# Two-layer streaming encoder on one core: how the relative-bias rows reach HBM, how they are read back, and when the constants are loaded

## The chip, the core and the metric

The kernel runs on one core of a Trainium2 chip. The core has five engines that run side by side: TensorE (PE in the profile, with its weight loads as PEld), VectorE (DVE), ScalarE (ACT), GpSimd (POOL) and SyncE (SP). Sixteen DMA engines move data between HBM and the on-chip memory; the kernel hands them transfers from SP, ACT and POOL, and the profile counts each issuer as a queue (q1 for SP, q0 for POOL, q10 for ACT). The metric is the device time of one execution in microseconds (us).

## What is computed

Two layers work on 256 tokens of width 2048. Each makes one wide input projection, three groups of attention heads, and an output projection that is added to `x`. Group C, the differential attention, has the relative-position bias that this change is about: four heads, one 32-entry table per head, the same table in both layers.

```python
for l in range(DEPTH):                                   # 2 layers
    h = _rms_norm(x, norm_g[l])
    proj = jnp.einsum('bsd,dn->bsn', h, w_in[l])         # 2048 -> 7238 columns
    ...                                                  # groups A (6 heads), B (6 heads)
    # group C, 4 heads, per block of 128 queries q0..q1_
    rel = jnp.arange(q1_)[None, :] - jnp.arange(q0, q1_)[:, None]
    bias = jnp.transpose(rel_bias[_t5_bucket(rel)], (2, 0, 1))
    mask = _chunk_mask(q0, q1_)                          # chunks of 64 tokens
    s1 = einsum(q1, k1) * scale + bias
    s2 = einsum(q2, k2) * scale + bias
    w = softmax(where(mask, s1, -inf)) - lam * softmax(where(mask, s2, -inf))
    ...
    x = x + jnp.einsum('bsm,md->bsd', mixed, w_out[l])
return _rms_norm(x, final_norm_g)
```

The bias depends only on key minus query, so one row of 511 values per head holds all of it. A tile of 128 queries needs that row shifted by one element from partition to partition.

## The kernel before

**Weights.** The weights (about 154 MB over both layers) stream once through the core. They are packed in HBM in the order of use, cut into parts of 512 KB (some of 384 or 454 KB). `load_to` issues each part's transfer from SP into a ring of four `raw` buffers; `split_to` turns a part into a high half `whi` (ACT, L146) and a low half `wlo` (DVE, L147), in rings of five buffers. `take()` hands the next part to the matmuls, and `after()` splits ahead and calls `tick()`, which runs the small steps that `later(n, ...)` has put off by n parts. So the order of all work is fixed by the order of the parts, `layer_slots()`: `n0` (8 parts), `cq0`..`cq3`, `ckv0`, `ckv1`, then head after head of group A as `aq`, `ak`, `ag`, then `n1`, group C as `dq`, `dk`, group B, and `wo0`..`wo15`. SP's transfer of part i waits until part i-4 has been split, since they share a buffer.

**Start.** `x` (2 MB) is loaded in pieces between the first eight parts (`load_start`, L160), and becomes `h` by `chunk_hi` (ACT, L293) and `chunk_lo` (DVE, L296). The first product is `pjL0n` (L392 to L394). Nine dummy matmuls, `ps_idle` (L232), run before it. In `split_start` POOL issues four transfers of constants: `cst` (512 KB: masks, identity, triangle, rotary tables), `rowt` (12 numbers copied to 128 partitions), `relt` (the bias table) and `onet` (which table entry each distance has, 64 KB). They stand under the fourth and eighth part in program order, but nothing precedes them on POOL. First users: `ps_st` (L304) reads a column of `cst`, `post_n0` (L472) reads `rowt`, and `rel_task` (L318) reads `relt` and `onet`.

**Bias rows.** `rel_task`, put off by 21 parts, multiplies `relt` by `onet` into a 4x512 tile, negates it (`relrow`, L320) and has POOL write it to the HBM tensor `reld` 128 times for each head. The source of that transfer lies in four partitions, one for each head. `relative(h)`, called from `post_dq`, later reads `reld` into a 128x384 tile in two transfers (columns 0 to 128 for the first block of queries, 128 to 384 for the second) with a row step of 511, so that each partition is one element further left. Two memsets on POOL then write the masked corners. `scores` adds the two column ranges (`BLK`) to the products on DVE (L748). `decay` is the same for group A and builds its tile on DVE.

Of the kernel before, what the change touches and what calls it, by code (L numbers as in the profile page):

```python
# [10 lines left out]
F32 = mybir.dt.float32  # L11
# [5 lines left out]
P = 128  # L17
D = 2048
S = 256
# [3 lines left out]
NA, NB, NC = 6, 6, 4  # L23
# [4 lines left out]
BIG = 1.0e30  # L28
# [59 lines left out]
BLK = ((0, slice(0, 128)), (1, slice(128, 384)))  # L88
# [7 lines left out]
def trunk(ctx: ExitStack, tc: tile.TileContext, xT, ws, cols, rows, relw, csts, oneh, out):  # L96
    nc = tc.nc
# [4 lines left out]
    tp = ctx.enter_context(tc.tile_pool(name="tmp", bufs=2))  # L102
    dr = ctx.enter_context(tc.tile_pool(name="dr", bufs=1, space=bass.MemoryType.DRAM))
# [7 lines left out]
    V, A, G, T = nc.vector, nc.scalar, nc.gpsimd, nc.tensor  # L111
# [6 lines left out]
    def load_to(r):  # L118
        while st["load"] <= min(r, len(PARTS) - 1):
            i = st["load"]  # L120
            off, w = PARTS[i]
            t = wp.tile([P, MAXW], F32, tag="raw", name=f"raw{i}", bufs=RB)
            src = ws[off:off + P * w].rearrange("(p f) -> p f", p=P)
            n = 2 if i == 0 else 1
            for j in range(n):
                if i < 8:
                    load_start(i, j, n)
                c = slice(j * w // n, (j + 1) * w // n)
                nc.sync.dma_start(out=t[:, c], in_=src[:, c])
            raw_t[i] = t  # L130
            st["load"] += 1

    def split_to(j):
        while st["split"] <= min(j, len(PARTS) - 1):
            i = st["split"]
            w = PARTS[i][1]
            load_to(i)
            hi = wp.tile([P, MAXW], F32R, tag="whi", name=f"whi{i}", bufs=HB)
            lo = wp.tile([P, MAXW], F32R, tag="wlo", name=f"wlo{i}", bufs=HB)
            src = raw_t.pop(i)[:, :w]  # L140
            n = 2 if i == 0 else 1
            for j in range(n):
                if i < 8:
                    split_start(i, j, n)
                c = slice(j * w // n, (j + 1) * w // n)
                A.activation(hi[:, c], src[:, c], AF.Copy)  # L146
                V.tensor_tensor(out=lo[:, c], in0=src[:, c], in1=hi[:, c].bitcast(F32), op=ALU.subtract)  # L147
            if 5 <= i < 10:
                square_start(i - 5)
            half_t[i] = (hi, lo)  # L150
            load_to(i + RB)
            st["split"] += 1
# [11 lines left out]
    def square_start(i):  # L164
        q = [x0[:, 4 * j:4 * j + 4, :] for j in range(4)]
        if i < 4:
            A.activation(q[i], q[i], AF.Square)
            if i % 2:
                V.tensor_tensor(out=q[i - 1], in0=q[i - 1], in1=q[i], op=ALU.add)
        else:  # L170
            V.tensor_tensor(out=q[0], in0=q[0], in1=q[2], op=ALU.add)
            V.tensor_tensor(out=x0[:, 0:2, :], in0=x0[:, 0:2, :], in1=x0[:, 2:4, :], op=ALU.add)
            V.tensor_tensor(out=x0[:, 0, :], in0=x0[:, 0, :], in1=x0[:, 1, :], op=ALU.add)
            X_now.sq = x0[:, 0, :]

    def split_start(i, j, n):
        for c in range(2 * i + j, 2 * i + j + 2 // n):
            xc = x0[:, c, :]
            X_now.chunk_hi(c, xc)
            X_now.chunk_lo(c, xc)  # L180
        if i == 3:
            G.dma_start(out=cst, in_=csts)
            G.dma_start(out=rowt, in_=rows[:, :2 * NA].to_broadcast([P, 2 * NA]))
        elif i == 7:
            G.dma_start(out=relt, in_=relw)
            G.dma_start(out=onet, in_=oneh)


    clock = [0]
# [2 lines left out]
    def later(dt, fn):  # L192
        tasks.append((clock[0] + dt, fn))
# [15 lines left out]
    def take():  # L209
        j = nexth[0]  # L210
        nexth[0] += 1
        split_to(j)
        return half_t.pop(j)

    def after():
        split_to(nexth[0] - 1 + HB - 1)
        tick()
# [3 lines left out]
    cst = const.tile([P, NCST], F32, name="cst")  # L221
    rowt = const.tile([P, 2 * NA], F32, name="rowt")
    relt = const.tile([32, NC], F32, name="relt")
    onet = ap_.tile([32, 512], F32, tag="rb", name="onet")
# [19 lines left out]

    x1d = dr.tile([KC // 4, P, 1024], F32, name="x1d")
    cumd = dr.tile([NA, S], F32, name="cumd")
    reld = dr.tile([NC, P, 512], F32, name="reld")

    def load_x(l, g, eng):
        t = ap_.tile([P, 4, S], F32, tag="v", name=f"xg{l}_{g}", bufs=3)  # L250
# [65 lines left out]
    def rel_task():  # L316
        p = psm.tile([P, 512], F32, tag="psm", name="ps_rel")
        T.matmul(p[:NC, :], lhsT=relt, rhs=onet, start=True, stop=True)  # L318
        t = ap_.tile([NC, 512], F32, tag="v", name="relrow", bufs=3)
        A.activation(t, p[:NC, :], AF.Copy, scale=-1.0)  # L320
        G.dma_start(out=reld, in_=t.unsqueeze(1).to_broadcast([NC, P, 512]))

    def lam_task():
        lamt = ap_.tile([P, 2 * 4 * 64], F32, tag="v", name="lamt", bufs=3)
# [16 lines left out]
    class Layer:  # L341
# [224 lines left out]
            self.post_k("a", h, ps)  # L566

        def relative(self, h):
            self.bias["d", h] = b = tp.tile([P, 384], F32, tag="dec", name=f"rel{self.n}{h}")
            base = reld[:]  # L570
            for c0, n, first in ((0, 128, 255), (128, 256, 127)):
                G.dma_start(out=b[:, c0:c0 + n],
                            in_=bass.AP(base.tensor, base.offset + h * P * 512 + first, [[511, P], [1, n]]))
            G.memset(b[0:64, 64:128], BIG)
            G.memset(b[0:64, 320:384], BIG)

        def post_dq(self, h, ps):
            self.relative(h)
# [131 lines left out]


        def decay(self, h):
            self.bias["a", h] = b = tp.tile([P, 384], F32, tag="dec", name=f"dec{self.n}{h}")
            cq = [self.cumq[:, t, h:h + 1] for t in range(2)]
            rows = self.cumb[:, h % 3, :]
            for o, t, k in ((0, 0, 0), (256, 1, 128)):
                V.scalar_tensor_tensor(out=b[:, o:o + P], in0=rows[:, k:k + P], scalar=cq[t], in1=maskA,
                                       op0=ALU.subtract, op1=ALU.add)
            V.tensor_scalar(out=b[:, P:2 * P], in0=rows[:, 0:P], scalar1=cq[1], scalar2=None, op0=ALU.subtract)
            if h == 2:  # L720
                self.cum_rows(3)

        def scores(self, grp, h, qk, hi, lo):

            n = f"{self.n}{grp}{h}"
            rows = [slice(0, 64), slice(64, 128)] if grp == "d" else [slice(0, P)]
            if grp == "b":
                bias = (maskB[:, P:], maskB)
            else:
                b = self.bias.pop((grp, h))  # L730
                bias = [b[:, c] for _, c in BLK]
            ss, ms = [], []
            for i, r in enumerate(rows):
                ps = pss.tile([P, 512], F32, tag="pss", name=f"pss{n}_{i}")
                prods = [(0, qk[r, 0:P], qk[r, S:S + P])]
                for a, b in ((hi, hi), (hi, lo), (lo, hi)):
                    prods.append((1, a[r, 0:P], b[r, P:384]))
                if grp == "b":
                    prods.insert(1, (0, self.qrT[:, h // 2, :], self.krT[:, h % 2, :]))
                    for a, b in ((self.qrh, self.krh), (self.qrh, self.krl), (self.qrl, self.krh)):  # L740
                        prods.append((1, a[:, h // 2, :], b[:, h % 2, :]))
                for j, (t, a, b) in enumerate(prods):
                    T.matmul(ps[:, BLK[t][1]], lhsT=a, rhs=b, start=(j == 0 or prods[j - 1][0] != t),
                             stop=(j + 1 == len(prods) or prods[j + 1][0] != t))
                s = tp.tile([P, 384], F32, tag=f"s{i}", name=f"s{n}_{i}")
                m = tp.tile([P, 2], F32, tag=f"nm{i}", name=f"nm{n}_{i}")
                for t, c in BLK:
                    V.tensor_tensor_reduce(out=s[:, c], in0=ps[:, c], in1=bias[t], scale=1.0, scalar=FLT_BIG,  # L748
                                           op0=ALU.add, op1=ALU.min, accum_out=m[:, t:t + 1])
                ss.append(s)  # L750
                ms.append(m)
            later(1, lambda: self.exps(grp, h, ss, ms))
# [151 lines left out]
    for l in range(L):  # L904
        lay = Layer(l, X_now)
        go = []
        later(9, lambda: go.append(lay.stat()))
        later(10, lambda: go.pop()())
        if l == 0:
            later(15, lam_task)  # L910
            later(21, rel_task)
        for name in layer_slots():
            if name == "wo0":
                lay.begin_out()
            lay.run(name)
        X_now = lay.xn
# [101 lines left out]
```

## Time and profile before

| | us |
|---|---|
| median of 3 runs | 933.56 |
| range of the runs | 931.06 to 933.9 |
| the profiled execution, its own time | 934.17 |
| span of its trace, first to last instruction | 932.4 |

| engine | busy us | share of the span |
|---|---|---|
| PE | 903.6 | 97% |
| PEld | 797.2 | 86% |
| DVE | 617.3 | 66% |
| ACT | 482.5 | 52% |
| POOL | 206.3 | 22% |

Times in the trace count from the span's first instruction. 1.8 us of the execution lie outside the span. A matmul's busy time is modelled and overlaps the next one's, so a stretch is better judged by where PE's instructions start and by the idle time in front of them than by its busy share. [...]

### The profile page before, as it was taken

What the parts mean: (1) busy time and instruction counts of PE and PEld (TensorE: products, weight loads), DVE (VectorE), ACT (ScalarE), POOL (GpSimd) and SP (SyncE); (2) the same over time, 40 slices, a digit from 0 to 9 for tenths busy, and PEclk for the clock granted to TensorE, in tenths of its full rate; (3) what the DMA queues carried; (4) which work ended last, traced back from release to release, by engine and by line L of the source; (5) the groups of instructions that cost most, each with busy time, mean ns of one, the idle gap of its engine ahead of it and who ended that gap; (6) DMA issues with size and microseconds to landing.
All of it is one profiled execution on the core that took longest, in us unless ns stands there. A gap on an engine that the chain in (4) does not pass through costs nothing.

```text
span 932.4 us, 14297 instructions
## 1 busy us (share of the span) xinstructions
PE 903.6 (97%) x5267; PEld 797.2 (86%) x5267; DVE 617.3 (66%) x1137; ACT 482.5 (52%) x877; POOL 206.3 (22%) x294
## 2 busy tenths in 40 slices
PE   8999589999999999999999999999999999999994
PEld 6888479888888999888888888988888899988884
DVE  5877266675676776777766676667567677676554
ACT  6554244444555665644555554445445566565441
POOL 1151000000412320346542400000041232032220
PEclk8999889999999999999999999999999999999997
DMA  9556455555664445677664555665456545565542
GB/s 312 189 188 145 92 166 196 190 177 159 195 197 152 136 152 177 214 217 232 209 223 163 195 168 163 194 194 175 157 195 195 162 136 141 180 218 209 191 170 90
DMA packets 51429, 168.13 MB, mean 180 GB/s; under 512 B 6724, under 2 KB 9296, under 8 KB 51360
## 3 DMA queue, kind: packets, MB, share of 16 engines
q1 hardware_dynamic: 45888, 154.65, 52.0%
q0 software_dynamic: 4112, 11.37, 4.3%
q10 hardware_dynamic: 1360, 1.21, 0.4%
q8 instruction: 41, 0.67, 0.3%
q14 instruction: 28, 0.23, 0.1%
HBM read 161.95 MB, written 5.26 MB: 179 GB/s over the span
## 4 chain that ended last, share of the span: by engine, by line
PE 93%; DMA 4%; DVE 1%; POOL 0%; ACT 0%; SPq 0%; issue 0%; DVEq 0%; ACTq 0%
PE pjL0wo L376 6%; PE pjL1wo L376 6%; DMA raw<-in_ws 4%; PE pjL0wo L378 3%; PE pjL1wo L378 3%; PE pjL1bg L376 2%; PE pjL0bg L376 2%; PE pjL1ag L376 2%; PE pjL1ak L376 2%; PE pjL1aq L376 2%; PE pjL0ag L376 2%; PE pjL1n L394 2%; PE pjL0n L393 2%; PE pjL1n L392 2%; PE pjL1n L393 2%; PE pjL0n L394 2%
## 5 line engine op out<-in xcount | busy, mean ns | idle before, releaser
L147 DVE TENSOR_TENSOR wlo<-raw,whi 128x1024 fp32r<-128x1024 f32 (+4 forms) x303 | 362.5, 1206 | 129.0 <-ACT whi L146 125.5
L146 ACT ACTIVATE whi<-raw 128x1024 fp32r<-128x1024 f32 (+4 forms) x303 | 301.2, 1012 | 38.9 <-DMA raw<-in_ws 36.6
L624 POOL TENSOR_TENSOR m<-mL,m 128x256 fp32r<-128x256 f32 x32 | 29.1, 913 | 326.6 <-ACT m L623 326.6
L376 PE MATMUL pjL0wo<-m,whi 128*128 128x512 f32 x256 | 91.0, 400 | 0.1
L376 PE MATMUL pjL1wo<-m,whi 128*128 128x512 f32 x240 | 83.8, 393 | 0.1
L378 PE MATMUL pjL0wo<-m,wlo 128*128 128x256 f32 x256 | 71.9, 281 | 0.0
L378 PE MATMUL pjL1wo<-m,wlo 128*128 128x256 f32 x240 | 67.2, 280 | 0.0
L376 PEld LDWEIGHTS pjL0wo<-m,whi 128*128 128x128 f32 x256 | 48.1, 188 | 12.5 <-POOL m L624 0.7
L376 PEld LDWEIGHTS pjL1wo<-m,whi 128*128 128x128 f32 x240 | 44.9, 187 | 10.4 <-POOL m L624 0.7
L378 PEld LDWEIGHTS pjL0wo<-m,wlo 128*128 128x128 f32 x256 | 48.4, 189 | 0.0
L378 PEld LDWEIGHTS pjL1wo<-m,wlo 128*128 128x128 f32 x240 | 45.4, 189 | 0.0
L376 PE MATMUL pjL0ak<-h,whi 128*128 128x512 f32 x96 | 35.8, 411 | 6.1 <-ACT whi L146 6.1
L376 PE MATMUL pjL0ag<-h,whi 128*128 128x512 f32 x96 | 36.7, 420 | 3.7 <-ACT whi L146 3.7
L392 PE MATMUL pjL0n<-whi,h 128*128 128x454 f32 (+2 forms) x96 | 37.1, 386 | 2.7 <-ACT whi L146 2.7
L393 PE MATMUL pjL0n<-wlo,h 128*128 128x454 f32 (+2 forms) x96 | 37.0, 385 | 0.4 <-DVE wlo L147 0.4
L394 PE MATMUL pjL0n<-whi,h 128*128 128x454 f32 (+2 forms) x96 | 36.3, 379 | 0.0
L392 PE MATMUL pjL1n<-whi,h 128*128 128x454 f32 (+2 forms) x96 | 35.3, 368 | 0.0
L394 PE MATMUL pjL1n<-whi,h 128*128 128x454 f32 (+2 forms) x96 | 35.0, 365 | 0.0
L393 PE MATMUL pjL1n<-wlo,h 128*128 128x454 f32 (+2 forms) x96 | 34.9, 364 | 0.0
L376 PE MATMUL pjL1bg<-h,whi 128*128 128x512 f32 x96 | 34.6, 401 | 0.0
L376 PE MATMUL pjL0bg<-h,whi 128*128 128x512 f32 x96 | 34.5, 400 | 0.0
L376 PE MATMUL pjL1ag<-h,whi 128*128 128x512 f32 x96 | 34.3, 400 | 0.0
(563 smaller groups left out, 2433.9 us busy)
## 6 DMA issues: line engine op xcount, KB each, us to landing
raw<-in_ws SPq DMA_DIRECT2D x248, 512.0 KB, 4.1
raw<-in_ws SPq DMA_DIRECT2D x32, 384.0 KB, 3.4
raw<-in_ws SPq DMA_DIRECT2D x15, 454.0 KB, 5.0
xg<-in_xT POOLq DMA_DIRECT2D x4, 512.0 KB, 4.3
x1d<-xg POOLq DMA_DIRECT2D x4, 512.0 KB, 6.2
xg<-x1d POOLq DMA_DIRECT2D x4, 512.0 KB, 3.9
x<-in_xT SPq DMA_DIRECT2D x7, 256.0 KB, 7.2
cumbL<-cumd POOLq DMA_DIRECT2D x4, 384.0 KB, 4.9
```

What stands on the lines that cost most here:

```text
L146: A.activation(hi[:, c], src[:, c], AF.Copy)
L147: V.tensor_tensor(out=lo[:, c], in0=src[:, c], in1=hi[:, c].bitcast(F32), op=ALU.subtract)
L376: T.matmul(ps, lhsT=hi[:, w], rhs=act[:, k, :, :].rearrange("p s t -> p (s t)"), start=first, stop=False)
L378: T.matmul(ps[:, S:], lhsT=lo[:, w], rhs=act[:, k, 0, :], start=False, stop=last)
L392: T.matmul(pq[q][:, :width], lhsT=act[:, k, 0, t], rhs=hi[:, w], start=(k == 0), stop=False)
L393: T.matmul(pq[q][:, :width], lhsT=act[:, k, 0, t], rhs=lo[:, w], start=False, stop=False)
L394: T.matmul(pq[q][:, :width], lhsT=act[:, k, 1, t], rhs=hi[:, w], start=False, stop=(k == kc - 1))
L624: G.tensor_tensor(out=self.m[:, c, 1, :], in0=m, in1=self.m[:, c, 0, :].bitcast(F32), op=ALU.subtract)
```

## The change

1. `reld` is now `[P, NC * 512]`: 128 rows, each with all four heads' 512 values (8 KB). `rel_task` writes the 4x512 tile once, as one row, to a new HBM tensor `relr`, and a second transfer copies that row 128 times from HBM to HBM.
2. `relative` reads one 128x256 piece for each head, not two pieces with 384 columns. The second block of queries uses all 256 columns, the first the right half; one corner is masked by one memset. `decay` hands over its two column ranges itself, so that `scores` takes both kinds alike.
3. The four transfers of constants leave POOL and `split_start`. SP issues them in `load_to`, `cst` and `rowt` behind the transfer of part 7, `relt` and `onet` behind that of part 10.

```diff
@@ load_to
             raw_t[i] = t
             st["load"] += 1
+            if i == 7:
+                nc.sync.dma_start(out=cst, in_=csts)
+                nc.sync.dma_start(out=rowt, in_=rows[:, :2 * NA].to_broadcast([P, 2 * NA]))
+            elif i == 10:
+                nc.sync.dma_start(out=relt, in_=relw)
+                nc.sync.dma_start(out=onet, in_=oneh)
@@ split_start
-        if i == 3:
-            G.dma_start(out=cst, in_=csts)
-            G.dma_start(out=rowt, in_=rows[:, :2 * NA].to_broadcast([P, 2 * NA]))
-        elif i == 7:
-            G.dma_start(out=relt, in_=relw)
-            G.dma_start(out=onet, in_=oneh)
@@ HBM tensors
-    reld = dr.tile([NC, P, 512], F32, name="reld")
+    relr = dr.tile([1, NC * 512], F32, name="relr")
+    reld = dr.tile([P, NC * 512], F32, name="reld")
@@ rel_task
-        G.dma_start(out=reld, in_=t.unsqueeze(1).to_broadcast([NC, P, 512]))
+        G.dma_start(out=relr.rearrange("a (h t) -> (a h) t", h=NC), in_=t)
+        G.dma_start(out=reld, in_=relr.to_broadcast([P, NC * 512]))
@@ relative
-            self.bias["d", h] = b = tp.tile([P, 384], F32, tag="dec", name=f"rel{self.n}{h}")
+            b = tp.tile([P, 384], F32, tag="dec", name=f"rel{self.n}{h}")[:, :S]
+            self.bias["d", h] = (b[:, P:], b)
             base = reld[:]
-            for c0, n, first in ((0, 128, 255), (128, 256, 127)):
-                G.dma_start(out=b[:, c0:c0 + n],
-                            in_=bass.AP(base.tensor, base.offset + h * P * 512 + first, [[511, P], [1, n]]))
-            G.memset(b[0:64, 64:128], BIG)
-            G.memset(b[0:64, 320:384], BIG)
+            G.dma_start(out=b, in_=bass.AP(base.tensor, base.offset + h * 512 + 127, [[NC * 512 - 1, P], [1, S]]))
+            G.memset(b[0:64, 192:256], BIG)
@@ decay
-            self.bias["a", h] = b = tp.tile([P, 384], F32, tag="dec", name=f"dec{self.n}{h}")
+            b = tp.tile([P, 384], F32, tag="dec", name=f"dec{self.n}{h}")
+            self.bias["a", h] = [b[:, c] for _, c in BLK]
@@ scores
-                b = self.bias.pop((grp, h))
-                bias = [b[:, c] for _, c in BLK]
+                bias = self.bias.pop((grp, h))
```

POOL in the first layer, from the last step of `ckv1` (`ckvsq`) over the bias rows to the first two `m` (a finished head's low half, L624 before, L626 after). `cumb` is group A's row of sums, read back from HBM. Before:

```order
L649 TENSOR_TENSOR ckvsqL_671<-ckvsqL_671,lsL0ckv_752 128x256
L321 DMA reld<-relrow 512x1x512
L624 TENSOR_TENSOR m_1130<-mL_1131,m_1130 128x256
L535 DMA cumbL_1237<-cumd 128x768
L624 TENSOR_TENSOR m_1130<-mL_1323,m_1130 128x256
```

After:

```order
L651 TENSOR_TENSOR ckvsqL_672<-ckvsqL_672,lsL0ckv_753 128x256
L323 DMA relr<-relrow 4x512
L324 DMA reld<-relr 128x2048
L626 TENSOR_TENSOR m_1132<-mL_1133,m_1132 128x256
L538 DMA cumbL_1239<-cumd 128x768
L626 TENSOR_TENSOR m_1132<-mL_1325,m_1132 128x256
```

One transfer became two at the same place, and the second reads what the first wrote, so POOL waits between them; the rows behind are the same.

SP's queue from part 7's load on, where `raw` are the weight parts in order (part 7, 8 and so on). Before:

```order
L129 DMA raw_200<-in_ws 128x908
L129 DMA raw_223<-in_ws 128x1024
L129 DMA raw_246<-in_ws 128x1024
L129 DMA raw_270<-in_ws 128x1024
L129 DMA raw_295<-in_ws 128x1024
```

After:

```order
L129 DMA raw_199<-in_ws 128x908
L134 DMA cst<-in_csts 128x1024
L135 DMA rowt<-in_rows 128x12
L129 DMA raw_224<-in_ws 128x1024
L129 DMA raw_247<-in_ws 128x1024
L129 DMA raw_271<-in_ws 128x1024
L137 DMA relt<-in_relw 32x4
L138 DMA onet<-in_oneh 32x512
L129 DMA raw_296<-in_ws 128x1024
```

The four transfers that were POOL's first now stand between weight parts on SP; nothing else on SP changed its place.

## Rows read from the trace of the kernel before

**Rows 1.** The page: busy time, and the last chain's shares, by engine.
```profile
PE 903.6 (97%) x5267; PEld 797.2 (86%) x5267; DVE 617.3 (66%) x1137; ACT 482.5 (52%) x877; POOL 206.3 (22%) x294
...
PE 93%; DMA 4%; DVE 1%; POOL 0%; ACT 0%; SPq 0%; issue 0%; DVEq 0%; ACTq 0%
```
**Rows 2.** Who waited for whom, PE, 0 to 120 us: total, times, longest.
```profile
PE pjL0ak L376 <- ACT whi L146: 6.1, 2, 5.7
PE pjL0ag L376 <- ACT whi L146: 3.7, 2, 2.0
```
**Rows 3.** Stretches: length; PE, PEld, DVE, ACT, POOL busy (instructions); PEclk, DMA share, GB/s.
```profile
90.00:100.00 10.00, 5.30 (x34) 4.62 (x32) 1.89 (x11) 0.12 (x1) 0.00 (x0) 0.95 0.40 79
100.00:110.00 10.00, 7.34 (x26) 5.49 (x27) 4.00 (x8) 3.94 (x9) 0.00 (x0) 0.70 0.42 92
```
**Rows 4.** Transfers, 76 to 124 us: POOL's queue; issues, KB, us to landing.
```profile
q0 software_dynamic: 1040, 1.05, 19.4%
...
raw<-in_ws SPq DMA_DIRECT2D x9, 512.0 KB, 20.7
reld<-relrow POOLq DMA_DIRECT2D x1, 1024.0 KB, 46.8
```
**Rows 5.** Timeline of POOL: start, us, instruction [idle before <-releaser].
```profile
62.49 0.57 POOL L535 DMA_DIRECT2D cumbL<-cumd  x1 [1.67 <-DMA cumd<-cumrL]
...
76.83 1.14 POOL L321 DMA_DIRECT2D reld<-relrow  x1
128.71 0.73 POOL L624 TENSOR_TENSOR m<-mL,m 128x256 fp32r<-128x256 f32 x1 [50.74 <-ACT m L623]
```
**Rows 6.** Timeline of PE: the same stretch in layer 0 and in layer 1.
```profile
87.23 0.50 PE L304 MATMUL ps_lsL<-cst,cqsqL 128*128 128x1 f32 x4
...
100.99 0.79 PE L376 MATMUL pjL0ak<-h,whi 128*128 128x512 f32 x1 [5.69 <-ACT whi L146]
...
127.21 0.39 PE L376 MATMUL pjL0aq<-h,whi 128*128 128x512 f32 x1
...
549.64 0.50 PE L304 MATMUL ps_lsL<-cst,cqsqL 128*128 128x1 f32 x4
...
570.43 0.39 PE L376 MATMUL pjL1aq<-h,whi 128*128 128x512 f32 x1
```
**Rows 7.** The page's transfers: KB each, median us from issue to landing, whole span.
```profile
raw<-in_ws SPq DMA_DIRECT2D x248, 512.0 KB, 4.1
...
cumbL<-cumd POOLq DMA_DIRECT2D x4, 384.0 KB, 4.9
```
**Rows 8.** Timelines: ACT's first parts; PE's `n0` products in layer 0 and layer 1.
```profile
9.29 0.58 ACT L146 ACTIVATE whi<-raw 128x454 fp32r<-128x454 f32 x1 [0.39 <-DMA raw<-in_ws]
...
11.32 0.96 ACT L146 ACTIVATE whi<-raw 128x908 fp32r<-128x908 f32 x1
...
9.93 0.47 PE L392 MATMUL pjL0n<-whi,h 128*128 128x454 f32 x1 [2.67 <-ACT whi L146]
...
32.35 0.39 PE L376 MATMUL pjL0cq<-h,whi 128*128 128x512 f32 x1
...
476.48 0.37 PE L392 MATMUL pjL1n<-whi,h 128*128 128x454 f32 x1
...
496.27 0.39 PE L376 MATMUL pjL1cq<-h,whi 128*128 128x512 f32 x1
```
**Rows 9.** Stretches of the start, columns as in rows 3.
```profile
10.00:17.00 7.00, 6.57 (x16) 5.04 (x17) 6.11 (x11) 6.47 (x12) 0.00 (x0) 0.52 1.03 385
17.00:32.35 15.35, 15.35 (x75) 13.98 (x74) 14.23 (x20) 13.46 (x18) 0.00 (x0) 0.99 0.83 271
```
**Rows 10.** POOL's queue from 3 to 9 us: packets, MB, share of 16 engines.
```profile
q0 software_dynamic: 234, 0.58, 40.6%
```
**Rows 11.** PE's first use of `cst`; a wait for `relL` in layer 0.
```profile
35.17 0.50 PE L304 MATMUL ps_stL<-cst,x 128*128 128x1 f32 x4
...
POOL relL L574 <- DMA relL<-reld: 8.5, 4, 2.9
```

## The prediction

> **What bounds the kernel now.** I read the page first: PE is busy 97% of the span and holds 93% of the chain that ended last, the transfers 4% [rows 1]. So a change pays only where PE does not run on. The view of who waited for whom, for PE alone, puts nearly all of its idle time after the start into `ak` and `ag` of layer 0, 6.1 and 3.7 us, for `whi`, the high half of a weight part [rows 2]. The table by stretches shows where: from 90 to 110 us PE is busy 5.30 and 7.34 of each 10 us, its granted clock falls (0.95, 0.70), and the transfers move 79 and 92 GB/s [rows 3], against 385 GB/s at their fullest in the start [rows 9]. The waits end with ACT, but ACT itself waits for a transfer, so the next view is that of the transfers in that stretch: nine weight parts took a median of 20.7 us to land there [rows 4], and 4.1 us over the whole span [rows 7]. What is different there is one transfer, `reld<-relrow`, 1 MB, 46.8 us [rows 4], issued by POOL at 76.83 [rows 5]. It holds 19.4% of the 16 engines over 48 us [rows 4]: 0.194 x 16 x 48 = 149 engine-us, over 46.8 us about 3.2 engines at a time. Over the stretch the engines together are only 0.40 busy [rows 3], and still the parts are late; I read this as parts that wait for the few engines the copy holds while the rest stand idle. PE's first wait ended at 100.99 after 5.69 us [rows 6], so it began at 95.3, 17.3 us after the issue had ended (76.83 + 1.14 = 77.97): that is how long the parts already loaded and split covered PE.
>
> The second place is the start. PE's first half part is done at 9.93 - 2.67 = 7.26; it then waits 2.67 us for the second half's `whi`, which ACT could begin only at 9.29 when its load had landed [rows 8]. After that gap the clock stands at 0.52 from 10 to 17 us [rows 9]. POOL's queue, which in those us carries only the constants, takes 40.6% of the 16 engines from 3 to 9 us [rows 10].
>
> **The copy of the bias row.** What its removal is worth is read from the other layer, which runs the same instructions without such a transfer. From the first `ps_ls` to the first product of the third `aq` layer 0 takes 127.21 - 87.23 = 39.98 us, layer 1 takes 570.43 - 549.64 = 20.79 us [rows 6]. The difference, 19.2 us, is the whole price of the old transfer: PE's waits and the products at the lower clock behind them.
>
> In its place come two transfers. The small one, 8 KB from four partitions, has its nearest row in POOL's wait of 1.67 us between group A's small write and the read that follows [rows 5]; POOL waits about as long here. Queued behind on POOL is the `m` that before sat idle 50.74 us ahead of 128.71 [rows 5], so 2 us there cost nothing. The large one, 1 MB from HBM to HBM, has no row. From below, the nearest is a weight part: 512 KB in 4.1 us [rows 7], so about 8 us. Another is group A's row copied to 128 partitions, 384 KB in 4.9 us [rows 7], so 13 us by size. From above it is the old transfer: 149 engine-us, if each KB still costs an engine as much, are 9.3 us over 16 engines at once, and 46.8 us if it is no faster than before. Below 8 us I see no reason to go, and below nothing the cost can't be, since the copy only adds traffic. I take 10 us: the row of `cumb` is nearest, a row in HBM copied 128 times by POOL's queue. While it runs it shares the engines with the weights. If it took them wholly for 10 us, PE would still have 17.3 us of cover; up to there its cost is nothing, and beyond it each us costs one. The sum goes on with 0, the range with 0 to 5.
>
> [...]
>
> **The reads in group C.** Each of eight heads loses one transfer and one memset on POOL, and 64 KB. POOL's memsets waited 8.5 us for those transfers in layer 0 [rows 11], but PE's chain shows none of it, POOL's share of it is 0% and DVE's 1% [rows 1]. DVE adds the bias over the same column counts. So 0, between a gain of some tenths and a loss of some tenths if the larger read lands later than the two did; the first `sL0d` would then be late, and PE has the next weight part's products to run meanwhile.
>
> **The constants.** POOL's queue moved 0.58 MB from 3 to 9 us at 40.6% of 16 engines [rows 10]: 0.406 x 6 = 2.4 us of all engines, taken from the first parts. Without them the second half part's `whi` starts at 9.29 - 2.4 = 6.9 instead of 9.29, and part 1's at 8.9 instead of 11.32 [rows 8]. PE goes on at 9.93 - 2.4 = 7.5, nearly where its first half ends (7.26). From 9.93 to 32.35 PE ran the 90 remaining products of `n0`, 22.42 us. Layer 1 runs 96 of them in 496.27 - 476.48 = 19.79 us [rows 8], so 90 at full clock take 18.55 us. Between lie 3.9 us of lower clock and small waits. In the new start some waits remain: part 1's `whi` is ready at 8.9 + 0.96 = 9.9, its `wlo` a good us later, and PE is there at about 9; I estimate 2 us of waits in all. Then 7.5 + 18.55 + 2 = 28.05, a gain of 32.35 - 28.05 = 4.3 us, if the clock stays up. If it falls as before, the 22.42 us stay, and the gain is the 2.4 us of the shift. If everything is in time, 7.3 + 18.55 = 25.9 and the gain is 6.5. I take 4.3: the remaining gaps are shorter than the 2.67 us after which it fell.
>
> What hides the constants at their new place: `cst` goes out behind part 7, whose load waits until part 3 is split; PE reaches part 3 at about 7.5 + 1.2 + 2 + 2 x 2.5 = 15.7, an estimate from the numbers above. `ps_st` first needs `cst` at 35.17 [rows 11], some 31 us in the new run. Even at twice a weight part's 4.1 us to land that leaves 7. The weight parts behind them on SP come 1 to 2 us later (0.58 MB at 271 to 385 GB/s [rows 9]), at a place where the transfers are 0.83 busy and PE, fed by nine buffers, is the slower. `relt` and `onet` are needed only by `rel_task`, 21 parts on.
>
> [...]
>
> **The sum**, against the profiled execution: 934.17 - 19.2 - 4.3 = 910.7. That execution lies 0.6 above the median of the runs, so **910** is predicted.
>
> **Rivals.**
> - *The clock falls in the start all the same.* PE still meets gaps near 8 and 10 us, and the clock fell after one of 2.67 us. Gain 19.2 + 2.4: 912.
> - *The constants cost the same wherever they stand.* The bytes ahead of part 9 are unchanged and the engines are full up to 17 us (1.03 [rows 9]). If the start is bound by the sum of its bytes, it gains nothing: 915. Against it, PE lost its time before 10 us, ahead of the new place.
> - *The copy still holds the weights up, but less.* If it takes 22 to 32 us over all engines, PE stalls for 5 to 15 us after its 17.3 us of cover: 915 to 925.
> - *The copy is as slow as before and now slows all 16 engines.* All 128 rows are read from one 8 KB stretch of HBM, and each byte is also written there; no row shows such a copy. Its place is the same, 78 us on. A wholly blocked stream stalls PE for the copy's time less 17.3. Slower than before begins where the stall passes 19.2 + 4.3 = 23.5, so at a copy of 41 us; at 46.8 it is 934.2 - 23.5 + 29.5 = 940. For it speaks only that the row is missing; against it, group A's broadcast from HBM, 384 KB in 4.9 us, lands nearly as fast as a weight part [rows 7].
> [...]
>
> **How the numbers follow.** The forecast with the clock up 50%; the clock falls 24%; no gain in the start 9%; the copy partly in the way 8%; as slow as before 5%, a little over half of that slower than before; four engines 4%. The first three end between 907 (all in time: 934.2 - 19.2 - 6.5 = 908.5, less the 0.6 and a run's scatter) and 915; with 2 us for the scatter of the runs (931 to 934) the range is 906 to 917 and leaves 17% out. About 0.3%, 2.8 us, is what a measurement of this kernel can tell from no change. Four engines, at 930, would be split by it, as would the slow copy's better half. Faster by more: 0.94; within it: 0.03; slower: 0.03.
>
> **What would show it.** The stretch from `ps_ls` to the third `aq` in layer 0 takes about 20.8 us, as in layer 1, with no wait of `ak` or `ag` for `whi`; weight parts land in 4 to 6 us there; the new `reld` lands in about 10 us. In the start the second half part's `whi` begins near 7 and the first product of `cq` near 28; a clock at 0.5 after 10 us would show the first rival, a `cq` at 32 the second. Wrong would be: weight parts above 15 us behind the copy, or a wait of `ps_st` for `cst`.

## The result

| | before | after |
|---|---|---|
| median of the runs, us | 933.44 (931.06 to 933.9, 4 runs) | 910.52 (909.28 to 911.83, 4 runs) |
| profiled execution, us | 934.17 | 909.28 |
| span of its trace, us | 932.4 | 907.5 |

The ratio of the times is 0.9757, with a 95% interval of 0.9744 to 0.977: 2.4% faster. The profiled execution of after is the fastest of its four. One execution of consts_sp_early ran at a mean granted clock of 0.56 from end to end and took 1479.29 us; it is in none of the times and ratios below.

The two page lines that answer to [rows 1], and the line of weight parts that answers to [rows 7]: PE's chain has taken over nearly all that the transfers held, while a weight part lands as fast as before over the whole span.

```profile
PE 893.8 (98%) x5267; PEld 791.3 (87%) x5267; DVE 616.8 (68%) x1137; ACT 482.8 (53%) x877; POOL 198.5 (22%) x275
...
PE 97%; DVE 1%; DMA 1%; POOL 0%; SPq 0%; ACT 0%; issue 0%; DVEq 0%; ACTq 0%
...
raw<-in_ws SPq DMA_DIRECT2D x248, 512.0 KB, 4.0
```

**The stretch behind the bias rows.** The view of who waited for whom, PE of after, 0 to 120 us (total, times, longest), has three entries, all of the start. The waits of `ak` and `ag` [rows 2] are gone:

```profile
PE ps_idle L233 <- DVE warm L237: 1.3, 1, 1.3
PE pjL0n L396 <- DVE wlo L154: 0.7, 1, 0.7
PE pjL0n L395 <- ACT whi L153: 0.2, 1, 0.2
```

The table by stretches (columns as in [rows 3]; PEclk is the clock granted to TensorE, as a share of full speed) shows PE full, its clock at 1.00, and the transfers moving 206 and 169 GB/s instead of 79 and 92:

```profile
90.00:100.00 10.00, 10.00 (x62) 8.78 (x61) 7.43 (x17) 5.96 (x9) 0.00 (x0) 1.00 0.63 206
100.00:110.00 10.00, 10.00 (x61) 8.89 (x61) 6.83 (x17) 4.88 (x11) 0.74 (x1) 1.00 0.57 169
```

Transfers from 65 to 90 us (KB each, median us to land). The copy lands in 7.9 us instead of 46.8, and the weight parts beside it in 4.7 instead of 20.7 [rows 4]:

```profile
raw<-in_ws SPq DMA_DIRECT2D x8, 512.0 KB, 4.7
reld<-relr POOLq DMA_DIRECT2D x1, 1024.0 KB, 7.9
relr<-relrow POOLq DMA_DIRECT2D x1, 8.0 KB, 3.9
```

POOL's timeline, answering to [rows 5]: between the two transfers POOL waits 3.61 us, and its next step is still idle 27 us ahead of its input, so the wait costs nothing.

```profile
76.28 0.55 POOL L324 DMA_DIRECT2D reld<-relr  x1 [3.61 <-DMA relr<-relrow]
103.98 0.74 POOL L626 TENSOR_TENSOR m<-mL,m 128x256 fp32r<-128x256 f32 x1 [27.15 <-ACT m L625]
```

**The start.** PE's timeline, the starts that answer to [rows 6], [rows 8] and [rows 11] (the last column of waits is empty where PE ran on):

```profile
7.33 0.47 PE L395 MATMUL pjL0n<-whi,h 128*128 128x454 f32 x1
...
9.28 0.47 PE L395 MATMUL pjL0n<-whi,h 128*128 128x454 f32 x1 [0.23 <-ACT whi L153]
...
10.42 0.47 PE L396 MATMUL pjL0n<-wlo,h 128*128 128x454 f32 x1 [0.66 <-DVE wlo L154]
...
27.64 0.39 PE L379 MATMUL pjL0cq<-h,whi 128*128 128x512 f32 x1
...
30.45 0.50 PE L306 MATMUL ps_stL<-cst,x 128*128 128x1 f32 x4
...
82.52 0.50 PE L306 MATMUL ps_lsL<-cst,cqsqL 128*128 128x1 f32 x4
...
103.31 0.39 PE L379 MATMUL pjL0aq<-h,whi 128*128 128x512 f32 x1
```

The second half part's products begin at 7.33 (9.93 before), those of part 1 at 9.28. ACT's first splits, against 9.29 and 11.32 in [rows 8], and the stretch that answers to [rows 9], where the clock was 0.52:

```profile
6.46 0.58 ACT L153 ACTIVATE whi<-raw 128x454 fp32r<-128x454 f32 x1 [0.36 <-DMA raw<-in_ws]
...
8.27 0.96 ACT L153 ACTIVATE whi<-raw 128x908 fp32r<-128x908 f32 x1 [0.23 <-DMA raw<-in_ws]
```
```profile
10.00:17.00 7.00, 6.58 (x32) 6.02 (x33) 6.82 (x13) 6.47 (x12) 0.00 (x0) 1.00 1.03 409
```

**Where the 24.9 us of the profiled executions come from.** `cq` begins 32.35 - 27.64 = 4.71 us earlier, and so does `ps_ls` (87.23 - 82.52). From `ps_ls` to the third `aq` layer 0 now takes 103.31 - 82.52 = 20.79 us instead of 39.98, which gives 19.19; layer 1 takes 20.79 as before. Together 23.90. The last 1.0 us lies behind the change's places, 0.9 of it behind the final norm's first product (14.0 us to the end of the span before, 13.1 now).

### The profile page after: what moved, and what is told of

Same layout as the page of the kernel before. It is cut to its first block, busy times and chain, and to the rows that moved or that the text cites. A ratio compares the mean times of both kernels' runs of the same rounds, so it can differ in the third digit from the quotient of the medians.

```text
span 907.5 us, 14276 instructions
## 1 busy us (share of the span) xinstructions
PE 893.8 (98%) x5267; PEld 791.3 (87%) x5267; DVE 616.8 (68%) x1137; ACT 482.8 (53%) x877; POOL 198.5 (22%) x275
## 3 DMA queue, kind: packets, MB, share of 16 engines
q10 hardware_dynamic: 1360, 1.21, 0.4%
## 4 chain that ended last, share of the span: by engine, by line
PE 97%; DVE 1%; DMA 1%; POOL 0%; SPq 0%; ACT 0%; issue 0%; DVEq 0%; ACTq 0%
PE pjL0wo L379 6%; PE pjL1wo L379 6%; PE pjL0wo L381 3%; PE pjL1wo L381 3%; PE pjL0bg L379 2%; PE pjL1bg L379 2%; PE pjL0ag L379 2%; PE pjL1ag L379 2%; PE pjL0aq L379 2%; PE pjL0ak L379 2%; PE pjL1ak L379 2%; PE pjL1aq L379 2%; PE pjL1n L397 2%; PE pjL1n L395 2%; PE pjL1n L396 2%; PE pjL0n L396 2%
## 5 line engine op out<-in xcount | busy, mean ns | idle before, releaser
L626 POOL TENSOR_TENSOR m<-mL,m 128x256 fp32r<-128x256 f32 x32 | 29.1, 913 | 303.5 <-ACT m L625 303.5
L379 PE MATMUL pjL0ag<-h,whi 128*128 128x512 f32 x96 | 34.3, 400 | 0.0
L379 PE MATMUL pjL1ag<-h,whi 128*128 128x512 f32 x96 | 34.3, 400 | 0.0
L379 PE MATMUL pjL1ak<-h,whi 128*128 128x512 f32 x96 | 33.8, 394 | 0.0
```

Source lines behind the costliest of these rows:

```text
L379: T.matmul(ps, lhsT=hi[:, w], rhs=act[:, k, :, :].rearrange("p s t -> p (s t)"), start=first, stop=False)
L626: G.tensor_tensor(out=self.m[:, c, 1, :], in0=m, in1=self.m[:, c, 0, :].bitcast(F32), op=ALU.subtract)
```

## The experiments

Each edit is against the changed kernel where nothing else is said. The mark "stretch" is the time from the first `ps_ls` to the third `aq` in layer 0: 39.98 us before, 20.79 after.

### One part alone

**consts_only**: the kernel before, with only the constants moved behind parts 7 and 10 on SP.

> The kernel before with only the third part of the change: the four transfers of constants are issued by SP behind parts 7 and 10; the bias rows are written and read as before. If the two gains are separate and additive, the first product of cq starts at 27.6 us as in the changed kernel, the stretch from ps_ls to the third aq in layer 0 stays at 40 us, and the time falls by 4.7 us, to about 928.8 (ratio 0.995). If the start is bound by the sum of its bytes, whoever issues them, cq starts at 32 and the time stays at 933.4. If the old copy, now starting 4.7 us earlier, stalled PE more because less is loaded ahead, the time would be above 929.

927.55 us (926.92 to 927.65) beside 932.01 of before; ratio 0.9954 (0.9939 to 0.9969). `cq` starts at 27.77; the stretch still takes 39.87 us, and the old copy lands as late as before:

```profile
reld<-relrow POOLq DMA_DIRECT2D x1, 1024.0 KB, 46.7
```

**copy_only**: the changed kernel, with the four constant transfers back on POOL in `split_start`.

> The kernel before with only the first two parts: the row is written once, copied from HBM to HBM, and read as one piece for each head; POOL issues the constants at the start as before. If the gains are separate, the stretch from ps_ls to the third aq in layer 0 takes 20.8 us, cq starts at 32.35 and the time falls by 19.2 us, to about 914.3 (ratio 0.979). A rival: part of the 19 us came from the constants (weights further ahead); then the stretch is longer than 20.8 and the time above 915.

912.52 us (910.95 to 913.34); ratio 0.9792 (0.9777 to 0.9807). The stretch takes 20.79 us, but `cq` starts at 32.75, and the clock falls from 10 to 17 us as it did before:

```profile
10.00:17.00 7.00, 6.26 (x15) 4.79 (x16) 5.83 (x10) 6.29 (x12) 0.00 (x0) 0.55 1.02 388
```

The parts add: 0.46% and 2.08% make 2.54%, beside 2.43% for both. Each works at its own place, as the prediction had it.

### What made the old copy slow

The prediction named the few engines that the old copy held, about 3.2 at a time [rows 4]; what could make them few is the shape, four rows outermost. The rival: the place that is read, four neighbouring partitions of the on-chip memory.

**copy_heads_out**: the copy stays from HBM to HBM, but with the four heads as its outer dimension, the shape of the old copy.

```diff
-        G.dma_start(out=reld, in_=relr.to_broadcast([P, NC * 512]))
+        G.dma_start(out=reld.rearrange("p (h t) -> h p t", h=NC),
+                    in_=relr.rearrange("a (h t) -> (a h) t", h=NC).unsqueeze(1).to_broadcast([NC, P, 512]))
```

> The changed kernel, but the copy from HBM to HBM runs over the heads outermost, 4 x 128 x 512, so that only its shape is that of the old copy and its source is HBM. If the old copy was slow because it had only four engines, this one holds four engines just as long: 1 MB lands in about 45 us, weight parts in about 20, and the 19 us of stall come back, about 929. If the old copy was slow because it read 1 MB out of four partitions of on-chip memory, this one takes at the rate of a weight part (512 KB in 4.1 us over 16 engines) 4 x 8 = 33 us at most on four engines and down to 8 us if the shape does not matter; with 17 us of cover the stall is then between 0 and 10 us, 910 to 920.

908.42 us (907.69 to 908.75); ratio 0.9748 (0.9731 to 0.9764), and PE waits for nothing from 60 to 140 us. Transfers from 70 to 100 us (POOL's queue: packets, MB, share of 16 engines; then the copy):

```profile
q0 software_dynamic: 1072, 1.06, 10.2%
...
reld<-relr POOLq DMA_DIRECT2D x1, 1024.0 KB, 16.5
```

The four-row shape takes twice as long to land as the 128-row shape (7.9) and costs nothing. It holds 0.102 x 16 x 30 = 49 engine-us, where the old copy held 149. So the shape by itself isn't what stalled PE.

**copy_from_sbuf**: no `relr`; the row is copied straight from the on-chip tile, with 128 rows as the outer dimension, one transfer for each head.

```diff
-        G.dma_start(out=relr.rearrange("a (h t) -> (a h) t", h=NC), in_=t)
-        G.dma_start(out=reld, in_=relr.to_broadcast([P, NC * 512]))
+        for h in range(NC):
+            G.dma_start(out=reld[:, h * 512:(h + 1) * 512].unsqueeze(0),
+                        in_=t[h:h + 1, :].unsqueeze(1).to_broadcast([1, P, 512]))
```

> The changed kernel, but without the row in HBM: POOL issues four transfers, one for each head, each from one partition of the on-chip tile to 128 rows of the HBM tensor, rows outermost. The source is that of the old copy, the shape is that of the new one. If the number of engines made the old copy slow, the four land in about 10 us together and the time is that of the changed kernel, 910.5. If reading 1 MB out of four neighbouring partitions made it slow, they need about 45 us again, now holding all 16 engines: the stall comes back and is 19 us or more, 930 or above, slower than the kernel before if all engines are held as the four were.

935.65 us (934.72 to 935.98); ratio 1.0041 (1.0026 to 1.0056): slower than before, although the constants' gain is in it. PE's wait for `whi`, then the transfers from 72 to 118 us, the landing times of everything that touches `reld` (the longest is a piece of the copy), and the stretches:

```profile
PE pjL0ak L380 <- ACT whi L153: 23.8, 1, 23.8
```
```profile
q0 software_dynamic: 320, 1.05, 75.0%
...
raw<-in_ws SPq DMA_DIRECT2D x6, 512.0 KB, 21.7
reld<-relrow POOLq DMA_DIRECT2D x4, 256.0 KB, 26.5
```
```profile
DMA to landing us min/median/max: 2.8/3.8/38.8
```
```profile
90.00:100.00 10.00, 1.32 (x11) 1.09 (x9) 0.00 (x0) 0.00 (x0) 0.00 (x0) 0.77 0.95 48
100.00:110.00 10.00, 0.00 (x0) 0.00 (x0) 0.00 (x0) 0.00 (x0) 0.00 (x0) 0.50 0.98 48
```

POOL's queue now holds 0.75 x 16 x 46 = 552 engine-us, the engines are 0.95 and 0.98 busy, and together they move 48 GB/s. The slowest of the four pieces landed after 38.8 us: 1.05 MB / 38.8 us = 27.0 GB/s. The old copy, from the same four partitions, moves 1.05 MB / 46.8 us = 22.4 GB/s [rows 4]. So 552 / 38.8 = 14 engines in the mean read little faster than 3.2 did; they only took nearly all engines from the weights instead of a few. That these busy engines waited for their source is an inference; the profile doesn't show what they waited for.

**rows_apart** and **rows_step4**: the old copy from the on-chip tile, heads outermost, on top of consts_only, but with the four source rows in partitions 0, 32, 64, 96 and in 0, 4, 8, 12 (the table is loaded into spread columns of a zeroed `relt`, so that the product puts the rows there). For rows_apart:

```diff
-                nc.sync.dma_start(out=relt, in_=relw)
+                nc.sync.dma_start(out=relt[:, 0:P:32], in_=relw)
...
-        T.matmul(p[:NC, :], lhsT=relt, rhs=onet, start=True, stop=True)
+        T.matmul(p, lhsT=relt, rhs=onet, start=True, stop=True)
...
-        G.dma_start(out=reld, in_=t.unsqueeze(1).to_broadcast([NC, P, 512]))
+        G.dma_start(out=reld, in_=t[0:P:32, :].unsqueeze(1).to_broadcast([NC, P, 512]))
```

> The kernel with only the constants moved (label consts_only), where the old copy still reads its four rows on chip; here these four rows lie in partitions 0, 32, 64 and 96, not in 0 to 3, and nothing else of the copy differs. If neighbouring partitions share one read path, and that path made the old copy slow, four rows apart land in about the 16.5 us of the copy from HBM over the same four engines, the stall goes, and the ratio to the kernel before is about 0.975. If each single partition is slow to read by itself, or four engines are slow with on-chip sources, it lands in about 46 us and the ratio is that of consts_only, 0.995.

> The kernel of label rows_apart, with the four rows in partitions 0, 4, 8 and 12 instead of 0, 32, 64 and 96. Rows in 0 to 3 landed after 46.7 us, rows 32 apart after 26.9 us, the copy from HBM over four engines after 16.5 us. If distance alone matters, rows 4 apart lie between the first two, 27 to 47 us. [...] The ratio to the kernel before stays at 0.976 either way up to 27 us.

rows_apart: 910.09 us (908.2 to 911.67), ratio 0.9757 (0.973 to 0.9785). rows_step4: 910.68 us (909.49 to 913.79), ratio 0.9754 (0.9736 to 0.9773). In both the stretch takes 20.79 us and PE waits for nothing from 60 to 140 us. Transfers from 70 to 100 us, of rows_apart and then of rows_step4:

```profile
q0 software_dynamic: 1040, 1.05, 15.1%
...
raw<-in_ws SPq DMA_DIRECT2D x10, 512.0 KB, 10.1
reld<-relrow POOLq DMA_DIRECT2D x1, 1024.0 KB, 26.9
```
```profile
q0 software_dynamic: 1040, 1.05, 10.6%
...
raw<-in_ws SPq DMA_DIRECT2D x11, 512.0 KB, 4.6
reld<-relrow POOLq DMA_DIRECT2D x1, 1024.0 KB, 18.7
```

Shape, number of packets and bytes are those of the old copy; only the partitions differ. rows_apart landed between its two expectations, 16.5 and 46 us; rows_step4 landed sooner than the 27 to 47 us that distance alone would give. The partitions alone take the copy from 46.7 us (its time in consts_only) to 26.9 and 18.7, and its hold on the engines from 149 to 0.151 x 16 x 30 = 72 and 0.106 x 16 x 30 = 51 engine-us. The last is about what the same shape holds when it reads HBM (49). So by these runs four rows are read most slowly from partitions 0 to 3, and distance alone doesn't order the times: 26.9 us at a step of 32, 18.7 at a step of 4. Why the partitions matter no run shows.

### How much cover the copy has

**copy_x8**: seven more copies of the row, from HBM to HBM behind the first (8 MB in all), go to a tensor that nobody reads; work is only added.

```diff
+        for e in range(7):
+            G.dma_start(out=relx[e], in_=relr.to_broadcast([P, NC * 512]))
```

> [...] If a copy takes the engines wholly while it runs, as the prediction's bound took it, eight copies of 7.9 us are 63 us, and PE stalls for all of it beyond 17 us of cover: 46 us, 956. If the weights keep their share of each engine, they need some 151 GB/s of about 400 (six parts of 512 KB in 20.8 us), the copies take what is left and land after 35 to 45 us, weight parts land in 5 to 10 us, and PE does not stall: 910.5.

910.11 us (909.19 to 912.12); ratio 0.9762 (0.974 to 0.9783). PE's only wait from 60 to 140 us, the two queues from 80 to 100 us while the copies run, the transfers from 70 to 125 us, and the landing times of the seven:

```profile
PE pjL0ak L384 <- DVE wlo L154: 0.5, 1, 0.5
```
```profile
q0 software_dynamic: 753, 5.51, 68.3%
q1 hardware_dynamic: 556, 2.06, 31.1%
```
```profile
relx<-relr POOLq DMA_DIRECT2D x7, 1024.0 KB, 21.2
raw<-in_ws SPq DMA_DIRECT2D x12, 512.0 KB, 9.8
```
```profile
DMA to landing us min/median/max: 10.0/21.2/32.7
```

The copies took up to 32.7 us to land. The weight parts land at twice their usual time and still come in time: POOL's queue takes 68.3% of the engines, about 11 of 16, and leaves SP's 31.1%. Eight such copies from HBM cost PE 0.5 us here.

**two_reads**: group C reads its bias in two pieces again, with two memsets, from the new `reld`.

```diff
-            G.dma_start(out=b, in_=bass.AP(base.tensor, base.offset + h * 512 + 127, [[NC * 512 - 1, P], [1, S]]))
-            G.memset(b[0:64, 192:256], BIG)
+            for c0, n, first in ((0, 128, 255), (128, 256, 127)):
+                G.dma_start(out=b[:, c0:c0 + n],
+                            in_=bass.AP(base.tensor, base.offset + h * 512 + first, [[NC * 512 - 1, P], [1, n]]))
+            G.memset(b[0:64, 64:128], BIG)
+            G.memset(b[0:64, 320:384], BIG)
```

> The changed kernel, but group C reads each head's bias again in two pieces into 384 columns and masks two corners, from the new tensor. If the reads are off PE's path, as the prediction priced them, the ratio to the kernel before is that of the change, 0.976, and PE waits nowhere in group C. If the larger single read lands later and holds the first scores up, or the smaller number of transfers helped, this kernel differs from the changed one by more than 1 us.

911.81 us (911.02 to 911.83); ratio 0.9751 (0.9734 to 0.9767). The single read is worth nothing that can be measured.

### When the constants load, and from which queue

**consts_pool_late**: POOL issues all four, but only after it has copied one column of part 3's high half into `cst`.

```diff
+            if i == 3:
+                G.tensor_copy(out=cst[:, 0:1], in_=hi[:, 0:1].bitcast(F32))
+                G.dma_start(out=cst, in_=csts)
...
```

> The changed kernel, but POOL issues the four transfers of constants, as before, and does so only when part 3 is split: it copies one column of that part's high half into the constants' tile first and so waits for it. If their time alone counts, cq starts at about 27.7 and the ratio is that of the change, 0.975. If POOL as the issuer slows the engines, the start is late again by some us, up to 0.979.

910.72 us (908.77 to 912.49); ratio 0.9765 (0.9741 to 0.9788). The issue comes at 14.70 (after: 14.65, from SP) and `cq` at 27.99. At this late place it makes no difference who issues.

**consts_act_early**: ACT issues all four at its start, behind `colt`.

```diff
+    A.dma_start(out=cst, in_=csts)
+    A.dma_start(out=rowt, in_=rows[:, :2 * NA].to_broadcast([P, 2 * NA]))
+    A.dma_start(out=relt, in_=relw)
+    A.dma_start(out=onet, in_=oneh)
```

> The changed kernel, but the four transfers of constants go out at the start again, from ACT right behind the load of the columns; POOL and SP issue none. If it is their time that costs, the second half part is late again, cq starts at about 32.3 and the ratio to the kernel before is that of the copy alone, 0.979. If it was POOL's way of issuing them that slowed the engines, cq starts at about 27.7 and the ratio is 0.975. ACT itself is held for four issues of about 0.4 us, some of it ahead of its first work at 3.45; that may add up to 1 us.

911.64 us (910.77 to 914.11); ratio 0.9779 (0.9756 to 0.9802). `cq` starts at 29.93, between the two expectations, and the clock is 1.00 from 10 to 17 us. But ACT itself is late: its table load comes behind the four issues, at 4.31 us and not at 1.21 as in after, and PE's first product at 6.73 and not at 4.61:

```profile
4.31 1.28 ACT L235 ACT_TABLE_LOAD   x1 [4.31 <-DMA colt<-in_cols]
```
```profile
6.73 0.75 PE L392 MATMUL pjL0n<-whi,h 128*128 128x454 f32 x1 [2.15 <-ACT whi L146]
```

From its first product to `cq` PE takes 29.93 - 6.73 = 23.20 us, in after 27.64 - 4.61 = 23.03. So nearly all of the 2.3 us stands ahead of the first product, where ACT was held.

**consts_sp_early** and **consts_sp_early_2**, the same kernel twice: SP issues all four behind part 1.

```diff
-            if i == 7:
+            if i == 1:
...
-            elif i == 10:
```

> The changed kernel, but SP issues all four transfers of constants behind part 1, about 3.5 us after the start, so the same bytes go out early, though in the weights' own queue and behind the loads that PE's first two parts need. If only the time of the bytes counts, part 1 is late as it was before (its high half at 11.3) and cq starts at 30 to 32. If the harm came from bytes of another queue that overtake loads issued ahead of them, part 1 is as early as in the changed kernel (high half at 8.3), part 2 is about 2 us later, PE may wait for it by about 1 us, and cq starts at 27.6 to 29: ratio 0.976 to 0.977.

> The kernel of label consts_sp_early once more, since its profiled execution ran at about half the granted clock from end to end and its trace can't be laid beside the others. By the timed runs it keeps 0.9775 of the time before, 2 us above the change. If that is the early bytes in the weights' own queue, the trace shows part 1 as early as in the changed kernel (high half at 8.3), part 2's later by about 2 us (from 10.3 to 12.5), a wait of PE for it near 11 us, and cq starting at 28.5 to 30.

First: 914.1 us, ratio 0.9775 (0.9759 to 0.9791). Second, which the trace belongs to: 914.46 us (913.06 to 915.49), ratio 0.9797 (0.9774 to 0.9821). `cq` starts at 29.63. SP's issue of part 2's `x` comes at 6.31 instead of 3.56, behind the four issues, and ACT waits for it; PE meets three waits of 1.7 us in all for `whi` and three of 1.5 for `wlo`, yet the clock holds:

```profile
11.62 0.91 ACT L294 ACTIVATE h<-x,colt 128x256 fp32r<-128x256 f32 x2 [1.98 <-DMA x<-in_xT]
```
```profile
10.00:17.00 7.00, 5.30 (x23) 4.12 (x23) 4.94 (x9) 5.11 (x9) 0.00 (x0) 1.00 1.00 391
```

So `cq` starts at 32.35 and 32.75 with the constants early on POOL, at 29.6 to 29.9 early on ACT or SP, and at 27.5 to 28.4 late on SP or POOL, but for one trace. That the 2 us of ACT and SP are the price of the early bytes is not shown: in both runs the engine that issues is also held by the four issues. In the traces with the constants early, the clock fell only where POOL issued them. There the loads of the first parts were late: the 454 KB pieces issued in the first 9 us took a median of 8.5 us to land in before and 9.0 in copy_only, against 6.2 in after and 6.8 with the same bytes from ACT. Why POOL's early queue holds the second half part up longer (its `whi` at 9.29, against 7.07 behind ACT's) stays open.

The one trace is rows_step4's, the slowest of its four executions. With the constants late, part 1 came late all the same: PE waited 1.23 us for its `whi`, the clock fell, and `cq` started at 30.17:

```profile
10.00:17.00 7.00, 6.08 (x21) 5.18 (x22) 6.52 (x10) 6.53 (x13) 0.00 (x0) 0.76 1.05 405
```

So 2 us in the start of a single trace are at the edge of what can be told.

## Why the prediction was right, and which step was wrong

| term, us | predicted | measured |
|---|---|---|
| the old copy's stall | 19.2 | 19.19 |
| the new copy | 0 (10 to land) | 0 (7.9 to land) |
| POOL's wait between the two | 1.67, off the path | 3.61, off the path |
| the reads in group C | 0 | 0 |
| the constants | 4.3 | 4.71 |
| sum in the profiled execution | 910.7 | 909.28 |
| median | 910.0 | 910.52 |

The 1.4 us between the two sums are 0.4 of the constants and the 1.0 behind the change's places, which was not forecast. That the median still comes within 0.5 us is in part luck: the profiled execution of after lies 1.24 us below its median, that of before 0.73 above.

**The copy's price** was taken from layer 1, which runs the same instructions without the transfer, and hit to a tenth of a us. It did not need the cause.

**The cause, as named, was wrong.** That the old copy held about three engines stands: 149 engine-us [rows 4]. That the weight parts waited for just these engines stays an inference, since the profile doesn't tell the engines apart; it fits that the parts land sooner as the hold shrinks (20.7, 10.1 and 4.6 us at 149, 72 and 51 engine-us). Wrong was to make the small number of engines the culprit. With the four-row shape from HBM (copy_heads_out) 3.0 are held in the mean and there is no stall; with the 128-row shape from the on-chip tile (copy_from_sbuf) 14 are held and there is a longer one, 23.8 us. The source's partitions decide: by them alone the copy goes from 46.7 to 18.7 us (consts_only, rows_step4). That the new copy cost nothing came true because the change also moved its source to HBM.

The number of engines does go with the shape from the on-chip tile: the four-row copy held 3.2 in the mean [rows 4], the 128-row copy 552 / 38.8 = 14. From HBM the four-row copy held 49 / 16.5 = 3.0; the changed kernel's own copy held 0.085 x 16 x 30 = 41 engine-us, 41 / 7.9 = 5.2 engines in the mean; with seven more behind it (copy_x8) the copies held about 11. These means are what the runs showed; none shows the 16 engines at once of the prediction's 9.3 us, nor the four of its chances and of the expectations. With the 128 rows alone, without `relr`, the ratio is 1.0041.

**Two rivals** were judged on that wrong footing. A new copy over four engines, at 930, got 4%, but no run shows a copy on four; the nearest is copy_heads_out, four rows on 3.0 engines in the mean, and it comes at 0.9748 without a stall, so the price was wrong. "As slow as before and slows all 16 engines" was tied to HBM. It is nearest to what copy_from_sbuf does from the on-chip tile, with 14 engines held in the mean: the rule there, the copy's time less 17.3, gives 38.8 - 17.3 = 21.5 us; PE waited 23.8, and the stretch is 47.10 - 20.79 = 26.3 us longer, with products at the lower clock behind the wait.

**The cover** of 17.3 us was never needed, and "beyond it each us costs one" was too harsh: copies that took up to 32.7 us cost 0.5 us of waiting (copy_x8), because they left the weights 31.1% of the engines. That sentence stood on the condition that the copy takes the engines wholly, which these copies did not. The rival of a copy of 22 to 32 us, at 915 to 925, was too dear for the same reason.

**The constants.** The steps came as told: the second half part's `whi` at 6.46 (predicted 6.9), part 1's at 8.27 (8.9), `cst` issued at 14.65 (15.7), `ps_st` at 30.45 (31) with no wait; the loads came 0.4 to 0.6 us earlier than shifted by 2.4. PE went on at 7.33 (7.5), and its 90 products up to `cq` took 27.64 - 7.33 = 20.31 us, 1.76 more than the 18.55 at full clock, where 2 had been put; the profile lists 0.7 + 0.2 of that as waits. The rival of the falling clock did not occur in after. The reason given against it, that the gaps left are shorter than 2.67 us, is not borne out: the clock held through a wait of 2.15 us in consts_act_early and fell after waits of 1.23 and 0.66 in rows_step4. With the constants early on POOL it fell to 0.52 and 0.55, in both kernels that have them there.

**"Constants cost the same wherever they stand: 915"** fell: the same bytes late, from SP or POOL, start `cq` at 27.77 (consts_only) and 27.99 (consts_pool_late) instead of 32.35, and consts_only alone gains 0.46%. The change moved both who issues and when. At the late place the issuer makes little difference: `cq` starts at 27.64 from SP (after) and at 27.99 from POOL (consts_pool_late). At the early place no run separates the issuer from the time that its own issues take.

No kernel here is faster than the changed one by more than the intervals allow: copy_heads_out 0.9748, two_reads 0.9751 and rows_step4 0.9754 lie within those of 0.9757.

## What to carry to other kernels

Price a stall by the same stretch in a layer or a pass that doesn't have it (19.2 us from layer 1 here, 19.19 measured); that holds even when the explanation is wrong, which only a run that changes one thing can tell. Before a few on-chip rows are copied many times, look at which partitions hold them, and spread the rows or pass them through HBM once: 46.7 us to land from partitions 0 to 3, 18.7 from 0, 4, 8, 12, and 7.9 in the changed kernel; in copy_from_sbuf engines that showed 0.95 busy moved 48 GB/s, and the weight parts queued behind took 21.7 us to land. Bytes that nobody needs yet go behind the loads that the first products wait for; here `cq` then began 4.71 us earlier.

## What the runs showed of the hardware

- The same 1 MB, from four rows to 128 each, landed in 46.7 us from partitions 0 to 3 (consts_only), 26.9 from 0, 32, 64, 96, 18.7 from 0, 4, 8, 12, and 16.5 from HBM; from HBM in the 128-row shape in 7.9. It held 149, 72, 51, 49 and 41 engine-us (the last from the changed kernel's line below, POOL's queue from 70 to 100 us).

```profile
q0 software_dynamic: 176, 1.06, 8.5%
```

- Sixteen engines, 0.95 to 0.98 busy, moved 48 GB/s while POOL's queue read partitions 0 to 3 (copy_from_sbuf).
- While eight 1 MB copies within HBM ran beside the weight stream, they took 68.3% of the engines and the weights 31.1% (copy_x8, 80 to 100 us), and PE lost 0.5 us.
- The `wo` products with `whi` take 400 ns in the mean in layer 0 and 393 in layer 1 before; after it is the other way round, so 1.5 us change places and cancel. They take 400 in both layers in two_reads and 395 in both in copy_only, so this does not go with the change; no run shows its cause.
